# Rotating 96 images by a quarter turn: from the matrix engine to one strided block transpose on the vector engine

## The chip, the cores and the metric

The kernel runs on one core of one Trainium2 chip. The metric is device time in microseconds (us) of one execution; lower is better.

The words used: the DMA engines move data between the memory that holds input and output (DRAM) and SBUF, the memory that the compute engines work on; PSUM is the memory that TensorE, the matrix engine, writes in these kernels. VectorE and ScalarE are the vector and the scalar engine. A packet is one piece of a transfer as the profile counts it. A "4 KB run" or "8 KB run" is a contiguous stretch of one partition's bytes, and the run length its size; other runs are executions.

## The reference

```python
batch, c, h, w = 32, 3, 256, 256
x = np.random.randn(batch, c, h, w).astype(np.float32)
return np.rot90(x, k=1, axes=(-2, -1)).astype(np.float32)
```

That is, `out[h', w'] = x[w', 255 - h']` for each of the 96 images of 256 KB. 25.17 MB must be read and 25.17 MB written; nothing is computed.

## The kernel before

It loads groups of 8 images (2 MB, 4 KB contiguous for each partition), turns them with TensorE in two steps, and stores them. The first step transposes 128x128 pieces into PSUM; ScalarE casts the result to bf16 and moves it to SBUF; a second matmul with a permutation matrix reverses the order of partitions; VectorE copies the result from PSUM to SBUF.

```python
x_v4 = x.rearrange("b c (p d) w -> (b c) p d w", d=4)      # 4 rows = 4 KB per partition
GROUPS = [8] * 11 + [4, 2, 2]
...
for gi, G in enumerate(GROUPS):
    nc.sync.dma_start(out=S4[:], in_=x_v4[i0 : i0 + G].rearrange("(j q) p d w -> (q p) j d w", q=2))
    ...
    for j in range(G2):
        for d4 in range(4):
            for par in range(2):
                nc.tensor.transpose(p1pair_r[:, 1 - par, :, :, d4], S4_r[:, j, d4, :, par], identity)
        for q in range(2):
            nc.scalar.copy(out=bt[:], in_=p1pair[:, :, q, :])         # fp32 -> bf16
        ...                                                            # 4 matmuls with exch
        for hh in range(2):
            nc.vector.tensor_copy(out=U4[:, j, 2 * hh : 2 * hh + 2, :], in_=psum2[:, hh])
    ...                                                                # store, the last three groups deferred
```

## Time and profile before

| | before |
|---|---|
| median time, first series | 127.58 us (3 runs, 127.54 to 128.63) |
| profiled span | 125.8 us |
| TensorE / VectorE / ScalarE busy | 101.3 / 60.5 / 51.9 us |
| bytes moved, mean rate | 50.42 MB, 401 GB/s |
| DMA at 9 tenths or more | every slice but the first and the last |

How to read it: a busy share is an average, and three engines look well used. What decides is which of them is never free. That is the set of 16 DMA engines; the lines are in the prediction.

### The profile page before, as it was taken

What the parts mean: (1) busy time and instruction counts of PE and PEld (TensorE: products, weight loads), DVE (VectorE), ACT (ScalarE), POOL (GpSimd) and SP (SyncE); (2) the same over time, 40 slices, a digit from 0 to 9 for tenths busy, and PEclk for the clock granted to TensorE, in tenths of its full rate; (3) what the DMA queues carried; (4) which work ended last, traced back from release to release, by engine and by line L of the source; (5) the groups of instructions that cost most, each with busy time, mean ns of one, the idle gap of its engine ahead of it and who ended that gap; (6) DMA issues with size and microseconds to landing.
All of it is one profiled execution on the core that took longest, in us unless ns stands there. A gap on an engine that the chain in (4) does not pass through costs nothing.

```text
span 125.8 us, 1521 instructions
## 1 busy us (share of the span) xinstructions
PE 101.3 (81%) x576; PEld 63.0 (50%) x576; DVE 60.5 (48%) x96; ACT 51.9 (41%) x97; POOL 1.2 (1%) x10
## 2 busy tenths in 40 slices
PE   0029999999999999999995994897897699999500
PEld 0028556475576555655771761654654555755300
DVE  0000655565647744747445542842841945656520
ACT  4003363633653365336434435246246056336300
POOL 3000000000000000000000000000000000000000
PEclk9999999999999999999999999999999999999995
DMA  3999999999999999999999999999999999999993
GB/s 69 400 409 413 419 409 408 413 397 415 421 421 422 422 418 422 417 418 421 423 419 422 422 419 418 419 421 418 423 422 421 419 415 421 422 404 411 410 413 133
DMA packets 12742, 50.42 MB, mean 401 GB/s; under 512 B 448, under 2 KB 448, under 8 KB 12736
## 3 DMA queue, kind: packets, MB, share of 16 engines
q1 hardware_dynamic: 6368, 25.17, 49.7%
q10 hardware_dynamic: 6368, 25.17, 48.9%
q8 instruction: 4, 0.07, 0.2%
q14 instruction: 2, 0.02, 0.0%
HBM read 25.17 MB, written 25.17 MB: 400 GB/s over the span
## 4 chain that ended last, share of the span: by engine, by line
DMA 40%; PE 40%; DVE 7%; ACT 6%; issue 1%; DVEq 1%; ACTq 0%
DMA out_dram<-U 34%; PE p1pair L88 25%; PE psum L102 15%; DMA S<-in_x_dram 6%; ACT bt L96 6%; DVE U L111 4%; DVE U_tail L111 3%; DVEq L154 0%; ACTq L125 0%; DVEq L111 0%; ACTq L96 0%
## 5 line engine op out<-in xcount | busy, mean ns | idle before, releaser
L111 DVE COPY U<-psum 128x512 f32<-128x512 f32 x88 | 55.5, 684 | 56.7 <-PE psum L102 44.7
L96 ACT CAST bt<-p1pair 128x512 bf16<-128x512 f32 x96 | 50.6, 593 | 65.8 <-PE p1pair L88 65.8
L88 PE MATMUL p1pair<-identity,S 128*128 128x128 f32 x384 | 63.9, 305 | 8.8 <-DMA S<-in_x_dram 8.8
L88 PEld LDWEIGHTS p1pair<-identity,S 128*128 128x128 f32 x384 | 52.0, 209 | 30.2 <-issue 25.2
L102 PE MATMUL psum<-bt,exch 128*64 128x512 bf16 x192 | 45.0, 395 | 8.9 <-DVE U L111 7.0
L102 PEld LDWEIGHTS <-exch 128*64 128x64 bf16 x192 | 11.0, 107 | 25.4 <-DVE U L111 9.5
L111 DVE COPY U_tail<-psum 128x512 f32<-128x512 f32 x8 | 5.1, 685 | 3.1 <-PE psum L102 3.1
L96 ACT ACT_TABLE_LOAD x1 | 1.3, 1283 | 0.7 <-PEq L143 0.7
L49 POOL TENSOR_SCALAR_AFFINE_SELECT exch<-exch 128x64 bf16<-128x64 bf16 x2 | 0.4, 238 | 0.0
masks.py:199 POOL TENSOR_SCALAR_AFFINE_SELECT identity<-identity 128x128 f32<-128x128 f32 x1 | 0.3, 292 | 0.0
L48 POOL MEMSET exch<- 128x64 bf16 x2 | 0.2, 151 | 0.0
masks.py:197 POOL MEMSET identity<- 128x128 f32 x1 | 0.2, 204 | 0.3 <-POOLq L143 0.3
L143 POOL MEMSET const-bfloat16-1.0<- 128x1 bf16 x1 | 0.1, 101 | 0.0
L143 POOL MEMSET const-uint8-127<- 128x1 uint8 x1 | 0.1, 101 | 0.0
L143 POOL MEMSET const-float32-0.0<- 128x1 f32 x1 | 0.1, 98 | 0.2 <-issue 0.2
L143 POOL MEMSET const-float32-1.0<- 128x1 f32 x1 | 0.1, 98 | 0.0
## 6 DMA issues: line engine op xcount, KB each, us to landing
S<-in_x_dram SPq DMA_DIRECT2D x11, 2048.0 KB, 17.6
out_dram<-U ACTq DMA_DIRECT2D x11, 2048.0 KB, 18.4
S<-in_x_dram SPq DMA_DIRECT2D x1, 1024.0 KB, 16.8
S<-in_x_dram SPq DMA_DIRECT2D x2, 512.0 KB, 8.5
out_dram<-U_tail ACTq DMA_DIRECT2D x1, 1024.0 KB, 5.8
out_dram<-U_tail ACTq DMA_DIRECT2D x2, 512.0 KB, 5.1
```

The costliest lines, as they stand in the source:

```text
L48: nc.gpsimd.memset(e, 0.0)
L49: nc.gpsimd.affine_select(out=e, in_=e, compare_op=mybir.AluOpType.not_equal, fill=1.0, base=-(P - 1) + hh, pattern=[[2, P // 2]], channel ...
L88: nc.tensor.transpose(p1pair_r[:, 1 - par, :, :, d4], S4_r[:, j, d4, :, par], identity,)
L96: nc.scalar.copy(out=bt[:], in_=p1pair[:, :, q, :])
L102: nc.tensor.matmul(out=psum2[64 * q : 64 * q + 64, hh], lhsT=exchh[hh][:], rhs=bts[q][:], start=True, stop=True,)
L111: nc.vector.tensor_copy(out=U4[:, j, 2 * hh : 2 * hh + 2, :], in_=psum2[:, hh])
L143: nc = _bacc.Bacc("TRN2", target_bir_lowering=False, num_devices=1)
```

## The change

The intent is to do the whole rotation with VectorE's 32x32 block transpose, in fp32 and from SBUF to SBUF. With 8 rows per partition, an image of 256 rows fills exactly 32 partitions. A column `w = 8k + q` of the input becomes row `255 - w` of the output, which belongs to partition `31 - k`. So each 32x32 block (32 partitions by 32 values of k, at a fixed row r and a fixed q) only has to be transposed in place, with k and q read backwards. All TensorE, PSUM and ScalarE arithmetic goes.

```diff
-    x_v4 = x.rearrange("b c (p d) w -> (b c) p d w", d=4)
-    out_v4 = out.rearrange("b c (p d) w -> (b c) p d w", d=4)
-    GROUPS = [8] * 11 + [4, 2, 2]
+    R = 8
+    K = H // R
+    Q = P // K
+    x_v = x.rearrange("b c (k r) w -> (b c k) (r w)", r=R).rearrange("(g p) f -> g p f", p=P)
+    o_v = out.rearrange("b c (k r) w -> (b c k) (r w)", r=R).rearrange("(g p) f -> g p f", p=P)
+    in_pool = ctx.enter_context(tc.tile_pool(name="in_pool", bufs=12))
+    out_pool = ctx.enter_context(tc.tile_pool(name="out_pool", bufs=12))
-    ...   (identity, exchange matrices, PSUM pools, the group loop, the deferred stores)
+    for g in range(N // Q):
+        S = in_pool.tile([P, R * W], fp32, name="S")
+        nc.sync.dma_start(out=S[:], in_=x_v[g])
+        U = out_pool.tile([P, R * W], fp32, name="U")
+        src = S.rearrange("p (r k q) -> p q r k", r=R, q=R)[:, ::-1, :, ::-1]
+        dst = U.rearrange("p (q k r) -> p q r k", q=R, r=R)
+        nc.vector.transpose(dst, src)
+        nc.scalar.dma_start(out=o_v[g], in_=U[:])
```

More of the change, by code (lines that the diff above doesn't have):

```diff
@@ L5 @@
 import concourse.tile as tile
-from concourse import bass_utils, mybir
-from concourse.masks import make_identity
+from concourse import mybir
 from concourse._compat import with_exitstack
@@ L20 @@
     assert H == W == 256
+    N = B * C
     P = 128
-    N = B * C
-    x_v4 = x.rearrange("b c (p d) w -> (b c) p d w", d=4)
-    out_v4 = out.rearrange("b c (p d) w -> (b c) p d w", d=4)
-    GROUPS = [8] * 11 + [4, 2, 2]
-    assert sum(GROUPS) == N
-    assert all(g % 2 == 0 for g in GROUPS)
-    fp32 = mybir.dt.float32
-    bf16 = mybir.dt.bfloat16
-    const_pool = ctx.enter_context(tc.tile_pool(name="const", bufs=1))
-    in_pool = ctx.enter_context(tc.tile_pool(name="in_pool", bufs=4))
@@ L36 @@
-    bt_pool = ctx.enter_context(tc.tile_pool(name="bt_pool", bufs=4))
-    out_pool = ctx.enter_context(tc.tile_pool(name="out_pool", bufs=3))
-    tail_pool = ctx.enter_context(tc.tile_pool(name="tail", bufs=1))
-    psum1_pool = ctx.enter_context(tc.tile_pool(name="psum1", bufs=2, space=bass.MemoryType.PSUM))
-    psum2_pool = ctx.enter_context(tc.tile_pool(name="psum2", bufs=2, space=bass.MemoryType.PSUM))
-    identity = const_pool.tile([P, P], fp32)
-    make_identity(nc, identity)
-    exchh = []
@@ L46 @@
-    for hh in range(2):
-        e = const_pool.tile([P, P // 2], bf16, name=f"exch{hh}")
-        nc.gpsimd.memset(e, 0.0)
-        nc.gpsimd.affine_select(
-            out=e,
-            in_=e,
-            compare_op=mybir.AluOpType.not_equal,
-            fill=1.0,
-            base=-(P - 1) + hh,
-            pattern=[[2, P // 2]],
-            channel_multiplier=1,
-        )
-        exchh.append(e)
-    TAIL_N = 3
-    deferred_stores = []
-    i0 = 0
-    for gi, G in enumerate(GROUPS):
-        is_tail = gi >= len(GROUPS) - TAIL_N
-        G2 = G // 2
-        S4 = in_pool.tile([P, G2, 4, W], fp32, tag="S", name="S4")
-        nc.sync.dma_start(
-            out=S4[:],
-            in_=x_v4[i0 : i0 + G].rearrange("(j q) p d w -> (q p) j d w", q=2),
-        )
-        S4_r = S4.rearrange("pp j d (k par) -> pp j d k par", par=2)
-        if is_tail:
-            U4 = tail_pool.tile(
-                [P, G2, 4, W], fp32, tag=f"tail{gi}", name=f"U4_tail{gi}"
-            )
-        else:
-            U4 = out_pool.tile([P, G2, 4, W], fp32, tag="U", name="U4")
-        for j in range(G2):
-            p1pair = psum1_pool.tile([P, 2, 2, W], fp32, name="p1pair")
-            p1pair_r = p1pair.rearrange(
-                "k dd q (pt dquad) -> k dd q pt dquad", dquad=4
-            )
-            for d4 in range(4):
-                for par in range(2):
-                    nc.tensor.transpose(
-                        p1pair_r[:, 1 - par, :, :, d4],
-                        S4_r[:, j, d4, :, par],
-                        identity,
-                    )
-            bts = []
-            for q in range(2):
-                bt = bt_pool.tile([P, 2, W], bf16, name="bt")
-                nc.scalar.copy(out=bt[:], in_=p1pair[:, :, q, :])
-                bts.append(bt)
-            psum2 = psum2_pool.tile([P, 2, 2, W], fp32, name="psum2")
-            for hh in range(2):
-                for q in range(2):
-                    nc.tensor.matmul(
-                        out=psum2[64 * q : 64 * q + 64, hh],
-                        lhsT=exchh[hh][:],
-                        rhs=bts[q][:],
-                        start=True,
-                        stop=True,
-                    )
-            for hh in range(2):
-                nc.vector.tensor_copy(
-                    out=U4[:, j, 2 * hh : 2 * hh + 2, :], in_=psum2[:, hh]
-                )
-        if is_tail:
-            deferred_stores.append((i0, G, U4))
-        else:
-            nc.scalar.dma_start(
-                out=out_v4[i0 : i0 + G].rearrange("(j q) p d w -> (q p) j d w", q=2),
-                in_=U4[:],
-            )
-        i0 += G
@@ L124 @@
-    for s0, G, U4 in deferred_stores:
-        nc.scalar.dma_start(
-            out=out_v4[s0 : s0 + G].rearrange("(j q) p d w -> (q p) j d w", q=2),
-            in_=U4[:],
-        )
+    R = 8
+    K = H // R
+    Q = P // K
+    fp32 = mybir.dt.float32
+    x_v = x.rearrange("b c (k r) w -> (b c k) (r w)", r=R).rearrange("(g p) f -> g p f", p=P)
+    o_v = out.rearrange("b c (k r) w -> (b c k) (r w)", r=R).rearrange("(g p) f -> g p f", p=P)
+    in_pool = ctx.enter_context(tc.tile_pool(name="in_pool", bufs=12))
```

## The prediction

> **What bounds the kernel now.** I read the page's busy table first, then its slices, then the DMA view, and only then the waits and the chain.
>
> ```profile
> span 125.8 us, 1521 instructions
> PE 101.3 (81%) x576; PEld 63.0 (50%) x576; DVE 60.5 (48%) x96; ACT 51.9 (41%) x97; POOL 1.2 (1%) x10
> DMA  3999999999999999999999999999999999999993
> GB/s 69 400 409 413 419 409 408 413 397 415 421 421 422 422 418 422 417 418 421 423 419 422 422 419 418 419 421 418 423 422 421 419 415 421 422 404 411 410 413 133
> DMA packets 12742, 50.42 MB, mean 401 GB/s; under 512 B 448, under 2 KB 448, under 8 KB 12736
> ```
>
> The busy table tempts one to name TensorE (81%) as the bound. The slices say otherwise: the 16 DMA engines are at 9 tenths or more in every slice but the first and the last, and the traffic stays near 420 GB/s. The input and the output are 25.17 MB each, so 50.33 MB must cross whatever the engines do. The stretches by time bear this out: the DMA share is 1.02 or 1.03 from 40 to 110 us at 418 to 420 GB/s (over 1 because packet records overlap), while the busy time of every compute engine varies. Where TensorE is not full, it is held by the stores:
>
> ```profile
> DMA out_dram<-U 34%; PE p1pair L88 25%; PE psum L102 15%; DMA S<-in_x_dram 6%; ACT bt L96 6%; DVE U L111 4%; DVE U_tail L111 3%; DVEq L154 0%; ACTq L125 0%; DVEq L111 0%; ACTq L96 0%
> ...
> DVE U L111 <- DMA out_dram<-U: 12.0, 4, 3.8
> ```
>
> The first line is the chain that ended last by line, the second is from the list of waits (total us, times, longest). The chain mixes DMA and TensorE because the two run side by side with nearly the same rate; what refutes a TensorE bound is that the DMA has no idle time that a faster TensorE could fill.
>
> So I split the 125.8 us by DMA time. From finer stretches: 0.45 MB of kernel data had moved by 4.0 us (82 GB/s from 1.5 to 2.5 us, 197 to 3.0, 356 to 4.0, less 0.09 MB of instructions and tables), which is worth 1.1 us at 420 GB/s; the effective start is 2.9 us. The last bytes move at about 123.7 us (418 GB/s in 122 to 123, 270 in 123 to 124, 16 after). That leaves 120.8 us for 50.33 MB, or 416.7 GB/s, and 2.1 us of receipt and closing barrier. The measured median, 127.58, lies 1.8 us above the profiled span; I carry that over.
>
> [...]12736 less 448 packets carry 50.33 MB, so 4096 B each; 420/16 = 26.25 GB/s an engine is 156 ns a packet[...]. [...]No transpose of VectorE is in the trace before.[...]
>
> **The change, part by part.**
>
> *Removed.* All TensorE work (384 transposes of 305 ns, 192 exchanges of 395 ns on the page), the 96 ScalarE casts of 593 ns and the 96 VectorE evictions of 684 ns. All of it lies beside a full DMA. Worth: nothing directly. A first-tile effect remains: the first store was issued at 21.9 us because a whole 2 MB group had to be worked through. That does not cost DMA time either, since loads filled the interval.
>
> *Added.* 24 VectorE transposes of 128x2048 fp32 elements, each reading and writing with an innermost step of 8 elements, 32 bytes. [...]4.42 us, in all 106 us. That is my choice[...]. Is 4.42 us hidden? A tile needs 1 MB in and 1 MB out, 2.097 MB / 420 GB/s = 4.99 us of DMA. So VectorE at 4.42 us still keeps ahead, by 11%. First load landed: the 2 MB one landed at 8.64 us, 1 MB less is about 6.1 us. VectorE could end at 6.1 + 106 = 112 us if never starved, before the DMA's end.
>
> *Moved: buffers and the tail.* Twelve input and twelve output buffers of 1 MB; the order of waits of the changed kernel shows about four loads and four stores outstanding at once. Loads run alone until the first store, at about 6.1 + 4.4 + 1 = 11.5 us, so about 3.8 MB of loads lead. When the two queues then share evenly, that lead persists, and when the last load lands near 114 us some 3.8 MB of stores remain, 9 us of DMA. The last transpose (4.4 us) and its issue fit inside this. So the explicit deferred tail goes, and nothing is lost: the end is again the DMA's.
>
> *Transfers.* The total of bytes is unchanged. What changes is the contiguous run: 8 rows, 8192 B for each partition, where it was 4096 B. If one row becomes one packet, [...]427 GB/s for 16 engines. The trace before has an independent trace of this: the fastest of its eight 8192 B instruction-fetch packets took 308 ns, 26.6 GB/s, so 426 GB/s for sixteen.
>
> *Sum.* 50.33 MB / 426 GB/s = 118.1 us; plus 2.9 for the start, 2.1 for the end, 1.8 outside the span: 124.9 us. If the packets stay at 4 KB and the rate is an even 420, 119.8 + 6.8 = 126.6; if it is the old average of 416.7, 127.6.
>
> **The rivals.**
>
> (A) *Packets stay at 4 KB.* For: no load or store of the kernel before used a larger one, and I cannot see from the program how a row is cut. Against: the 8 KB instruction packets exist. It gives 126.6 to 127.6: the same. I give it 35 to 40%.
>
> (B) *VectorE becomes the bound.* The margin is only 4.42 against 4.99 us. If [...]5.5 us a tile, the end is 6.1 + 132 + 5 (last store and barrier) + 1.8 = 145 us[...]. For: [...]nothing measured before covers it[...]. [...]I give it 15%.
>
> (C) *VectorE is not slowed by stride*, 2.28 us a tile. The time is as in the main line, as DMA still bounds; only busy time drops to 55 us.
>
> (D) *The tail costs more.* The last load, transpose and store come in series: about 1 + 4.4 + 0.5 + 2.5 + 1.5 = 10 us from the last load's data to the end. If stores have overtaken, so that little is queued then, up to 5 us of DMA idle appear at the end: up to 130. Against: the lead computed above, 9 us of stores, covers it.
>
> **Range and chances.** The main line gives 124.9, rival A 126.6 to 127.6; a weight of 60 to 40 and a little for D makes 125.3. The line for faster by 2% is 125.0, so the main line falls almost on it: whether it is counted as faster hangs on a few tenths. [...]Range 122.3 to 129; the part above it is mainly B. Faster 0.43, same 0.41, slower 0.16.
>
> **What would show it.** In the profile after: the DMA row again at 9 from the second slice to the last but one, with 420 or more GB/s and a count of packets near 6144 large ones (main line) or 12288 (A). VectorE the only busy engine, with means of 4.4 us (my choice), 2.3 (C) or above 5 (B); in B the chain becomes VectorE from end to end and DMA falls below 9. The last store should be issued about 5 us before the end and no idle slice should precede it (D). The prediction is wrong if the transposes average above 4.9 us, or if the DMA rate moves out of 415 to 430 GB/s although the DMA stays full.

The 4.42 us for a strided transpose, the 2.28 us of rival C, the times of rival B and the fixed 151 ns that some expectations below use were my estimates: the trace before has no transpose on VectorE that could show them.

## The result, and the profile after

The changed kernel took 124.48 us (median of 4 runs, 124.43 to 124.65). In the same series the kernel before took 128.06 us (4 runs, 127.54 to 128.63). The ratio is 0.972, with a 95% interval of 0.968 to 0.976: faster by 2.8%. A ratio here is the mean time of one kernel's fast runs over that of the other's of the same rounds, so it is not quite the ratio of the medians. The result is exact in fp32, where the kernel before rounded to bf16.

The page of the changed kernel, with its span, busy time by engine, slices, DMA line and costliest group (line, engine, operation, shapes, count, then busy us, mean ns, and idle time before with its releaser):

```profile
span 122.7 us, 162 instructions
DVE 94.4 (77%) x24; POOL 0.2 (0%) x4
DMA  3999999999999999999999999999999999999995
GB/s 88 419 427 411 312 430 433 422 433 427 427 427 427 427 427 427 427 427 427 427 427 427 427 427 427 427 427 430 427 427 427 427 427 427 427 427 427 427 427 211
DMA packets 6912, 50.33 MB, mean 410 GB/s; under 512 B 768, under 2 KB 768, under 8 KB 768
...
L40 DVE STREAM_TRANSPOSE U<-S 128x2048 f32<-128x2048 f32 x24 | 94.4, 3958 | 21.2 <-DMA S<-in_x_dram 20.2
```

The DMA row is as full as before, and yet the span is 3.1 us shorter. The rate next to it differs: 427 GB/s where it was about 420. The packet line suggests the reason, which the experiments test: 6912 packets less 768 small ones are 6144, half as many as before, so 8192 B each. VectorE is busy for 94 us, but it waits for loads, so it is not the bound.

The same division of the span as in the prediction, now for both profiles (bytes by 4.0 us over the steady rate give the start; the last byte gives the end):

| part of the span | before | after |
|---|---|---|
| effective start of the data | 2.9 us | 2.45 us (0.664 MB moved by 4.0 us) |
| 50.33 MB | 120.8 us, 416.7 GB/s | 118.7 us, 424 GB/s |
| after the last byte | 2.1 us | 1.5 us |
| span | 125.8 us | 122.7 us |

One thing in the slices was not expected: a rate of 312 GB/s in the slice from 12.3 to 15.3 us. Without it the middle would take 50.33/0.427 = 117.9 us, so it costs 0.8 us.

### The profile page after: what moved, and what is told of

The parts are those of the page before. It is cut to its first block, busy times and chain, and to the rows that moved or that the text cites.

```text
span 122.7 us, 162 instructions
## 1 busy us (share of the span) xinstructions
DVE 94.4 (77%) x24; POOL 0.2 (0%) x4
## 2 busy tenths in 40 slices
DMA packets 6912, 50.33 MB, mean 410 GB/s; under 512 B 768, under 2 KB 768, under 8 KB 768
## 4 chain that ended last, share of the span: by engine, by line
DMA 86%; DVE 6%; SPq 1%; issue 0%; DVEq 0%
DMA S<-in_x_dram 73%; DMA out_dram<-U 13%; DVE U L40 6%; SPq L35 1%; DVEq L40 0%
## 5 line engine op out<-in xcount | busy, mean ns | idle before, releaser
L40 DVE STREAM_TRANSPOSE U<-S 128x2048 f32<-128x2048 f32 x24 | 94.4, 3958 | 21.2 <-DMA S<-in_x_dram 20.2
## 6 DMA issues: line engine op xcount, KB each, us to landing
S<-in_x_dram SPq DMA_DIRECT2D x24, 1024.0 KB, 19.6
out_dram<-U ACTq DMA_DIRECT2D x24, 1024.0 KB, 16.5
```

What stands on the lines that cost most here:

```text
L40: nc.vector.transpose(dst, src)
```

## The experiments

My theory was that the gain is the larger packet and not the new engine path. The rivals were that removing the TensorE path and its uneven demand for data gave the gain, that VectorE is not really hidden, and that transfer size or buffer count did it. Twelve kernels ran, in three series. The kernel before was run alongside each series, with medians of 128.21, 128.25 and 127.95 us.

### e1: the changed kernel with 4 KB runs

```diff
-        S = in_pool.tile([P, R * W], fp32, name="S")
-        nc.sync.dma_start(out=S[:], in_=x_v[g])
+        S = in_pool.tile([P, 2, H2 + 16], fp32, name="S")      # H2 = R * W // 2, a gap of 64 B
+        nc.sync.dma_start(out=S[:, :, :H2], in_=x_v[g].rearrange("p (h f) -> p h f", h=2))
     # U and the store likewise; the transpose as 2 x 2 pieces of 128x512
```

> The changed kernel with a gap of 64 B in the middle of each partition of both tiles, so that a load or store can only run 4 KB at a time; the transpose is cut in four (128x512 each) to fit. Theory (the gain is the larger packet): 12288 packets of 4 KB, 418 to 420 GB/s in the steady slices, 126.2 to 126.8 us. Rival (the gain is from removing the TensorE path and its uneven demand for data): the steady rate or the time stays that of the changed kernel, 124.2 to 124.8 us. The run e2 is its control.

Measured: 127.04 us (6 runs, 126.97 to 127.21), ratio to before 0.990 [0.987, 0.994]. Two lines of its page, the rate by slice and the packets:

```profile
GB/s 37 412 422 421 323 405 424 419 421 420 420 422 422 421 421 421 421 420 420 422 422 421 421 417 419 420 421 420 425 422 420 421 420 420 420 420 424 422 421 162
DMA packets 13057, 50.34 MB, mean 402 GB/s; under 512 B 768, under 2 KB 768, under 8 KB 13056
```

The steady rate is back at 420 to 421, with twice the large packets. The steady rate alone accounts for 50.33 MB/420 - 50.33 MB/427 = 2.0 us of the 2.5 us lost against e2. Another part is the start. The first slice has 37 GB/s where the changed kernel has 88, and issuing one load takes SyncE 540 ns (median) where it took 328 ns. By the division above the effective start is then at 2.9 us, as before the change. The kernel before, however, issued its loads in 368 ns (median) although they had four 4 KB runs for each partition, so the slow issue of e1 is not shown to come from the run length.

### e2: the control, four transposes and 8 KB runs

```diff
-        nc.vector.transpose(dst, src)
+        for hq in range(2):
+            for hr in range(2):
+                nc.vector.transpose(dst[:, 4*hq:4*hq+4, 4*hr:4*hr+4], src[:, 4*hq:4*hq+4, 4*hr:4*hr+4])
```

> The changed kernel with the transpose cut in four as in e1, but with the 8 KB runs kept. VectorE by the cost of the changed kernel (3967 ns less 151 ns for 2048 elements, so about 955 + 151 = 1105 ns for 512) has 4.4 us a tile, 106 us in all, still below 4.9 us of DMA a tile. Both theories: 124.2 to 124.9 us; if it is above 125.5, e1 must be read against this run and not against the changed kernel.

Measured: 124.50 us (4 runs, 124.44 to 124.56), ratio 0.970. The pieces took 1107 ns each, 98.3 us in all. That is less than the 106 us expected, because records of consecutive transposes overlap a little. The part that does not grow with the size, 151 ns in my expectation, comes out at (4 x 1107 - 3958)/3 = 157 ns with the whole transpose of the changed kernel, or at 150 ns with the medians of e1 (1104) and of the changed kernel (3967). Cutting the transpose costs nothing, so the difference of e1, 2.5 us, belongs to the cut runs and the gap that cuts them. The 2.0 us of steady rate belong to the run length, since the kernel before also moved about 420 GB/s, with 4 KB runs and no gap; the slower start is not separated from the gap.

### e3: the old engines with 8 KB runs

```diff
-            in_=x_v4[i0 : i0 + G].rearrange("(j q) p d w -> (q p) j d w", q=2),
+            in_=x_v8(x, i0, G),      # (b c k) (r w), 8 rows per partition, two 8 KB runs for 8 images
     # the stores likewise; GROUPS = [8] * 11 + [4, 4]; arithmetic unchanged, result wrong on purpose
```

> The kernel before with all its TensorE, ScalarE and VectorE work, but each partition loads and stores 8 KB runs (8 rows of a partition in order, 4 images per MB), last groups 4 and 4; the result is wrong on purpose, as the old arithmetic now meets other rows. Theory (packets): 6144 large packets, 426 to 428 GB/s where the DMA is full, 125.0 to 126.0 us, so most of the gain without the transpose. Rival 1 (the gain needs the new engine path): 127.3 to 128.6 us. Rival 2: TensorE, 101 us busy before, becomes the bound when the data comes faster; then the DMA share falls below 0.98 in the middle.

Measured: 125.99 us (6 runs, 125.95 to 126.43), ratio 0.983 [0.979, 0.986], which straddles the limit of 2% and counts as unclear, though it is clear of 1; the result was wrong, as intended. So 2.2 of the 3.7 us between before and e2 come with the old engines still at work. Its stretches by time show where most of the remaining 1.5 us may go (from:to, length, busy us of PE, PEld, DVE, ACT and POOL, then clock, DMA share and GB/s):

```profile
60.00:80.00 20.00, 16.77 (x97) 10.30 (x97) 10.35 (x17) 8.40 (x16) 0.00 (x0) 0.95 1.01 428
111.00:112.00 1.00, 1.00 (x8) 0.50 (x7) 0.30 (x2) 0.00 (x0) 0.00 (x0) 1.00 0.43 180
119.00:120.00 1.00, 0.00 (x0) 0.00 (x0) 0.22 (x1) 0.00 (x0) 0.00 (x0) 0.50 0.40 164
```

In the middle the DMA is full, at the same 428 GB/s. Near the end it has two holes, of 0.57 and 0.60 us by the DMA share, which the kernel before did not have (its emptiest microsecond from 110 to 123 us had a share of 0.92). In the first hole TensorE is busy for the whole microsecond; in the second the last store is just being issued. This fits an old path whose tail is no longer fast enough for the faster transfers: rival 2 is false for the middle, and may hold at the tail. One reservation: this kernel ends with groups of 4 and 4 images, the kernel before with 4, 2 and 2, so some of the holes may belong to the larger last group.

### e4: no transpose at all

```diff
-        nc.vector.transpose(dst, src)
-        nc.scalar.dma_start(out=o_v[g], in_=U[:])
+        nc.scalar.dma_start(out=o_v[g], in_=S[:])      # wrong result on purpose
```

> The changed kernel without the transpose: the loaded tile itself is stored (wrong on purpose). If VectorE is wholly hidden, 124.0 to 124.8 us, as in the changed kernel. Rival: the 4 us transpose costs something at the start and the end, or its SBUF traffic slows the DMA; then 121.5 to 123.5 us. It also shows whether the slow stretch of the loads at 12 to 15 us of the changed kernel (312 GB/s) comes from VectorE or from the start of the stores: with the stores starting about 4 us earlier, it should move to about 8 us in the second case and vanish in the first.

Measured: 124.54 us (6 runs, 124.48 to 124.60), ratio 0.971. A kernel that only copies is no faster than the one that rotates: VectorE is wholly hidden, start and end included. The slow stretch did not vanish. It moved with the stores, whose first issue is here at 5.59 us instead of 9.72:

```profile
GB/s 96 427 342 377 430 427 427 427 427 430 427 427 427 427 427 427 427 427 427 427 427 430 430 427 427 427 427 427 427 427 427 427 427 427 427 427 427 427 427 200
```

### e5: what the stride costs

```diff
-        nc.vector.transpose(dst, src)
+        # by turns: as before (L47); both dense (L49); source step 8 (L51); destination step 8 (L53);
+        # step 4 on both (L55); step 2 on both (L57); step 8 on both, not reversed (L59); tensor_copy, step 8 (L61)
```

> The changed kernel with the transpose of every tile replaced, in turn, by one of eight forms over the same 2048 elements (three tiles each, wrong on purpose): strided as in the kernel, with its reversed directions (3967 ns in the profile); dense on both sides; step 8 on the source alone; step 8 on the destination alone; step 4 on both; step 2 on both; step 8 on both without reversing; and a plain strided copy, step 8 on both. Theory of the prediction ([...]the two sides run in parallel): dense 2.28 us, each single side and step 4 as long as both, 3.97; step 2[...], near dense. Rival 1 (the sides add): a single side about 3.1 us. Rival 2 (stride is free and fp32 or the 32x32 block is slow): dense also 3.97 us. Rival 3 (the reversal costs): step 8 without reversal well under 3.97.

Measured: 124.38 us. Its output is wrong, which doesn't matter for the time. Its groups by form (busy us, mean ns, then idle before):

```profile
L47 DVE STREAM_TRANSPOSE U<-S 128x2048 f32<-128x2048 f32 x3 | 11.9, 3968 | 11.4 <-DMA S<-in_x_dram 11.4
L51 DVE STREAM_TRANSPOSE U<-S 128x2048 f32<-128x2048 f32 x3 | 11.8, 3943 | 5.2 <-DMA S<-in_x_dram 5.2
L55 DVE STREAM_TRANSPOSE U<-S 128x2048 f32<-128x2048 f32 x3 | 11.6, 3863 | 2.2 <-DMA S<-in_x_dram 2.2
L59 DVE STREAM_TRANSPOSE U<-S 128x2048 f32<-128x2048 f32 x3 | 11.6, 3860 | 7.8 <-DMA S<-in_x_dram 7.8
L53 DVE STREAM_TRANSPOSE U<-S 128x2048 f32<-128x2048 f32 x3 | 11.5, 3833 | 2.0 <-DMA S<-in_x_dram 2.0
L57 DVE STREAM_TRANSPOSE U<-S 128x2048 f32<-128x2048 f32 x3 | 6.9, 2313 | 2.0 <-DMA S<-in_x_dram 1.9
L49 DVE STREAM_TRANSPOSE U<-S 128x2048 f32<-128x2048 f32 x3 | 6.9, 2297 | 1.8 <-DMA S<-in_x_dram 1.8
L61 DVE COPY U<-S 128x2048 f32<-128x2048 f32 x3 | 6.0, 1997 | 3.3 <-DMA S<-in_x_dram 2.2 <-DMA out_dram<-U 1.1
```

The expected times held in every form of the transpose. Dense costs 2297 ns, close to the estimate of 2.28 us. Step 2 (2313 ns) is as good as dense. Step 4 (3863 ns) already pays the full price, and step 8 pays no more (3860 ns without the reversal). One strided side (3943 ns for L51, 3833 for L53) costs almost what two do (3968 for L47, 3860 for L59), so the costs of the two sides do not add. The reversal adds about 0.1 us at most (L47 against L59). The three rivals fall. The size differs from my estimate: if the 150 ns found with e1 holds for the dense form too, a strided element costs (3968 - 150)/(2297 - 150) = 1.78 times a dense one, where 4.42 us would make it 1.99.

The eighth form (L61) is a plain copy. It steps by 8 elements on both sides too, and took 1997 ns, less than even the dense transpose. So the runs show what the step costs this transpose; why it costs that is not shown. No dense copy was run, so whether a copy pays for its step is open.

### e6 and e7: how much slack VectorE has

```diff
         nc.vector.transpose(dst, src)
+        nc.vector.transpose(dst[:, :1], src[:, :1])      # e6: an eighth twice;  e7: [:, :4], a half twice
```

> The changed kernel with one eighth of each transpose done twice (same values again, so the result is right): about (3967 - 151)/8 + 151 = 628 ns more, 4.6 us of VectorE a tile, still under the 4.9 us of DMA (2.097 MB at 427 GB/s). Theory (VectorE has slack to the DMA's pace): 124.3 to 125.0 us. Rival (VectorE is already on the path at each tile): 24 x 0.63 = 15 us more, 139 us.

> As e6, but half of each transpose is done twice: 3816/2 + 151 = 2059 ns more, 6.03 us a tile, above the DMA's 4.9 us. Theory: VectorE is now the bound from the first tile to the last, 5.7 us to the first load, 24 x 6.03 = 145 us, some 7 us for the last store and the end, 1.8 us outside the span: 157 to 160 us, DMA share in the middle near 0.82. Rival (DMA and VectorE share something and add): 24 x 2.06 = 49 us more, 174 us.

Measured: e6 took 124.85 us (4 runs, 124.77 to 125.00) and e7 152.10 us (4 runs, 152.07 to 152.60), ratio 1.188; both results right. In e6 VectorE was busy for 108.5 us, 14 more than in the changed kernel, and the time rose by 0.4 us, inside the expected range. In e7 the chain changed hands; these are parts of its chain that ended last, by line and in order of time (start us, us, what):

```profile
DVE U L40 61%; DVE U L41 30%; DMA S<-in_x_dram 3%; DVEq L68 1%
...
75.58 7.65 DVE U L40 x2
83.23 3.88 DVE U L41 x2
```

VectorE is the bound from end to end. A tile takes (7.65 + 3.88)/2 = 5.77 us rather than the expected 6.03: consecutive transposes overlap, since their own records say 3.93 and 2.05 us. Hence 152 instead of 157 to 160 us. The expected DMA share in the middle, 0.82, was wrong too: it was 0.99 from 10 to 100 us and fell only later, because the twelve buffers let loads run ahead (the last was issued at 86.1 us). The mean over the span is 335 GB/s. The crossover thus lies between 4.5 us of VectorE a tile (e6, 108.5/24) and 5.8 us (e7), around the DMA's 4.9.

### e8: first loads from two queues

```diff
-        nc.sync.dma_start(out=S[:], in_=x_v[g])
+        (nc.scalar if g in (1, 3) else nc.sync).dma_start(out=S[:], in_=x_v[g])
```

> An attempt to beat the changed kernel: loads 1 and 3 are issued from ScalarE's queue, idle until 9.7 us[...]. In the changed kernel 106 GB/s move from 2 to 3 us and the full rate is reached after. If issuing limits that ramp: 0.3 to 0.6 us gained, 123.9 to 124.2 us, and more than 106 GB/s in 2 to 3 us. If the first packets' latency does (they took 0.8 to 1.3 us), nothing: 124.4 to 124.7 us.

Measured: 124.37 us (6 runs, 124.14 to 124.51), ratio 0.970. Between 2 and 3 us, 156 GB/s moved instead of 106. But the first tile landed later: the first transpose started at 7.7 us instead of 5.7, while the rate from 3 to 6 us was no higher (423 against 431 GB/s). The runs overlap those of the changed kernel, so a gain is not shown.

### e9: 2 MB transfers with 8 KB runs

```diff
-        S = in_pool.tile([P, R * W], fp32, name="S")
-        nc.sync.dma_start(out=S[:], in_=x_v[g])
+        S = in_pool.tile([P, 2, R * W], fp32, name="S")        # 6 buffers
+        nc.sync.dma_start(out=S[:], in_=x_v[2 * g:2 * g + 2].rearrange("t p f -> p t f"))
     # two transposes, then one store of 2 MB
```

> The changed kernel with loads and stores of two tiles (2 MB, as before the change), 6 buffers of each; the runs stay 8 KB, the transposes the same. Theory (the size of the packet counts, not that of the transfer): steady 427 GB/s, 124.3 to 125.2 us; the last store of 2 MB may show a little at the end. Rival (1 MB transfers are part of the gain): 125.8 us or more.

Measured: 124.24 us (6 runs, 124.19 to 124.33), ratio 0.971. It is 0.2 us below e10 of the same series (124.46, lowest 124.42), and no runs overlap. It has the lowest median; e8, in another series, had single runs as low (124.14). So the 1 MB transfers of the change gave no part of the gain.

### e10 and e11: four and two buffers

```diff
-    in_pool = ctx.enter_context(tc.tile_pool(name="in_pool", bufs=12))
-    out_pool = ctx.enter_context(tc.tile_pool(name="out_pool", bufs=12))
+    # e10: bufs=4 in both;  e11: bufs=2 in both
```

> The changed kernel with 4 buffers on each side in place of 12. As the trace shows four loads and four stores outstanding at most, and VectorE (4.0 us) runs ahead of the DMA (4.9 us a tile): 124.3 to 125.0 us. Rival (the deep buffers carry the lead that covers the tail): 1 to 4 us more, with an idle slice of the DMA at the end.

> As e10 with 2 buffers. A load then waits for the transpose two tiles earlier; two tiles take 4.0 us of transpose and about 6 to 7 us of load to landing: 5.0 to 5.5 us a tile, 130 to 142 us, with the DMA below full in the middle. If the rivals are right that buffers hardly matter, under 126 us.

Measured: e10 took 124.46 us (4 runs, 124.42 to 124.52), so eight of the twelve buffers buy nothing: in the changed kernel a load landed 19.6 us after its issue and a store 16.5 us (medians), 4.0 and 3.4 tiles of 4.9 us. e11 took 151.60 us (4 runs, 150.93 to 152.35), more than the 142 us that I allowed. From its list of waits (total us, times, longest):

```profile
DVE U L40 <- DMA out_dram<-U: 44.6, 22, 3.9
```

I had counted a load's landing as 6 to 7 us and thought of loads alone. With two output buffers, a transpose also waits for the store two tiles earlier, which lands 7.7 us (median) after its issue. That makes (3.97 + 7.7)/2 = 5.8 us a tile. From the first transpose at 5.5 us to the last at 141.2 us, 23 intervals, the trace has 5.9.

### e12: an experiment that did not come about

```diff
+    for g in reversed(range(N // Q)):      # after a loop that issues all 24 loads
+        nc.scalar.dma_start(out=o_v[g], in_=tiles[g][:])
```

> No transpose, 24 buffers; all loads are issued, and the stores only after the last load, the last tile first (wrong on purpose). If the DMA is bound by bytes and packets alone, loads alone and stores alone each run at 427 GB/s and the time is as in e4, 124.5 us, plus 1.5 to 3 us for the turn from loads to stores. If mixing both directions costs or helps, the rate of one half differs from 427. The slow stretch of about 3 us that follows the first stores in every run so far: if it comes from loads and the first stores together, it vanishes here; if from the first stores alone, it is there after the turn, near 62 us.

Measured: 124.55 us (4 runs, 124.44 to 124.61). Its output is wrong, which doesn't matter for the time. It tells nothing about its question: the first store was issued at 5.62 us, as in e4, while the load of the last tile, which the program stores first, was issued only at 96.3 us. The instructions were thus reordered when the kernel was built. It counts as a repeat of e4.

## Why the prediction was right or wrong

The prediction of 125.3 us, faster as the likeliest class, was right: 124.48 us lies inside the range and 0.4 us from the sum of its main line, 124.9. Some of this is luck. The class was close to a coin toss, at 0.43 against 0.41 for the same. The number 125.3 does not follow from its own weights: 0.6 x 124.9 + 0.4 x 126.6 is already 125.6, without D. And errors of the sum cancelled, as told below.

**The bound.** The DMA binds both kernels. After the change this is shown twice: by the full slices, and by e4, where taking the transpose away changes nothing.

**The packet.** The main line stood on one 8 KB row becoming one packet, at 426 to 427 GB/s. Both happened (8192 B a packet, 309 ns each by its records, 427 GB/s), and e1 shows the reverse. If a packet costs a fixed time and a time by its bytes, the rates of 420 and 427 GB/s, over 16 engines, put the fixed part at 2 x 156.0 - 307.0 = 5.1 ns, an estimate from these two rates alone. Rival A, which I gave 35 to 40%, was false. e1 also tells what it would have cost: 127.0 us.

**VectorE's 4.42 us.** This was my estimate, and no trace before the change showed it. That the step of 8 elements slows the transpose was right (3968 ns against 2297 dense, e5), the size off: 3.96 us on the page, as a strided element costs 1.78 times a dense one and not 1.99 times. Why the step costs time is not shown; the copy of e5 steps as far and took half the time (1997 ns). The error did not show in the total, because VectorE is hidden either way. The 2.28 us for a dense transpose, an estimate too, came out at 2297 ns. Rival B falls by e6 and e7, and rival C by e5.

**Start and end.** I carried over 2.9 and 2.1 us; they became 2.45 and 1.5. Why is open. At the start e1, with 4 KB runs, returns to 2.9, but e3 and e9, with 8 KB runs in loads of 2 MB, start at about 2.8 and 2.7 by the same division. At the end e1, with the new engines, has 1.9 us (125.3 less the last byte at 123.4).

**The slow stretch** of 0.8 us was not foreseen and cancels most of these two gains.

**The removed work: "Worth: nothing directly."** This step fell short. At equal 4 KB runs the new path was still 1.0% faster (e1), and at equal 8 KB runs the old path was 1.5 us slower than e2 (e3). At 8 KB holes in the DMA at the tail are seen, with the reservation told there. At 4 KB it is not settled. So the run length gave about 2 to 2.5 us of the 3.7 (e1, e3), and the rest went with the removed path. The profiled run of before was one of its fastest (127.58 us), only 0.5 us above e1. The rest is the spread of the old kernel, whose runs in the three series go from 127.41 to 129.12 us, while the changed kernel's stay within 0.22. What makes the old one spread was not tested, but the record shows what goes with it. Of its 33 runs in the three series, the seven with a granted TensorE clock of 0.960 or 0.961 took 128.66 to 129.12 us, and the eight with 0.983 or more took 127.41 to 128.21. So a slower TensorE may cost time that a DMA row of nines does not show; that the clock is the cause was not tested.

**The tail (rival D)** did not come: the DMA stayed at 418 GB/s or more until 121 us.

**Open:** the cause of the slow stretch (287 to 385 GB/s from 11 to 15 us in the changed kernel). It follows the first store in each profile looked at for it. The first store is issued at 5.6, 9.7 and 16.1 us in e4, the changed kernel and e9, and the rate falls about 1 to 3 us later. In the changed kernel only the loads' packets lengthen, from 309 ns to a mean of 437 to 482 ns in each half microsecond from 12 to 14 us. They do so before the first data packet of a store is recorded, at 13.9 us. So it seems to belong to the first stores or to their meeting with loads. e12 should have separated these and did not.

## What to carry to other kernels

When the DMA engines are full in every slice, the work of an engine beside them is worth little (about 1% here) until it makes a hole; look first at the packet line, where doubling the contiguous run per partition from 4 KB to 8 KB was worth nearly 2% here. Before replacing an engine by another, compare its time for each tile with the DMA's time for the same tile: the new one may be slow (4.0 us of stride-bound transpose) as long as it stays below (4.9 us). Four buffers did the work of twelve (124.46 us), but two did not (151.60 us).
